# A fifth inner pair in the first down projection, and another order of work around the first norm and in the tail

## The chip, the cores and the metric

One core of a Trainium2 chip runs the whole program once. The metric is the device time of one execution in microseconds (us). The kernel before took 1548.7 us (median of 3 runs, 1547.63 to 1548.96).

## What is computed

One step of a streaming encoder layer over 576 columns (512 frames of a new stream and 64 frames of a running one), model width 1024, hidden width 2816. Cut to what matters here:

```python
h = LN1(alpha*x + 0.5*FFN1(x))                                   # FFN1: (silu(x@Wg) * (x@Wu)) @ Wdown
z = h @ w_in  -> columns split among mLSTM q,k,v,o,i,f | attention q,k,v | branch gates g_m, g_a
h = LN2(alpha*h + w_out(sig(g_m)*P_m(mLSTM(h)) + sig(g_a)*P_a(BandAttn(h))))
y = LN3(alpha*h + 0.5*FFN2(h))
```

All is float32. Each matrix is split into a high part in the format that TensorE multiplies fast (fp32r) and a low part, the rest; a product is three matmuls, high by high, high by low and low by high.

## The kernel before

Everything is kept transposed: a tile is 128 features by 576 tokens. The two halves of the tokens are called A and B (columns 0 to 287 and 288 to 575). TensorE's order is written out by hand (the class `Order` counts the estimated time of the matmuls issued so far, and `later` sets a step due at a time of that count); the orders on ScalarE (ACT), VectorE (DVE), GpSimd (POOL) and SyncE (SP) are made by a scheduler at compile time out of priorities: an instruction counts as issued so many places earlier as its `high_priority` offset says (HOT is 300, the weight pump 30), and `issue_after` puts it behind a named one on the same engine. Every queue is then fixed, and an engine works through its own in order.

**Weights.** `plan` lists the weight chunks in the order of their use. `pump` (L232) loads a chunk into one of two raw buffers (`wr`, an SP transfer), then makes the high part (an ACT copy, `wh`) and the low part (a DVE subtraction, `wl`). There are four pairs of `wh` and `wl` (`NWB`); `done` gives a pair back when the last product with it has been issued. A raw buffer is free for the next load when both parts of its chunk have been made.

**The down projection of an FFN** (`ffn`, from L1290) sums 22 hidden tiles into 8 output tiles j. Hidden tiles 8 to 15, the inner ones, are multiplied for a pair of outputs (j, j+1) with seven block products in place of eight (`seven`, L1154): the blocks are two outputs by two groups of inner tiles (8 to 11 and 12 to 15) by two halves of the tokens. The products are a11, a12, t0, q1, q0, t1 and a22, in the order of the code; their weights stand in four chunks a, t, u and v, the last two made out of sums of the raw chunks. Each product runs over 4 inner tiles with three matmuls each. The other 14 hidden tiles are multiplied one by one (`plain`, L1136) in chunks of 8 and 6 (`DC`). For n = 1 the order is: plain for outputs 1 and 3 together, plain for 5, then for j = 0, 2, 4 `seven` and plain of j, then plain for 6 (half A) and 7, `seven` for 6, and plain for 6 (half B) at the end. `Inner` makes the sums of hidden tiles that the seven products need; `Hidden` makes the high and low parts of the hidden tiles in the order `ORDER`. Both take buffers of the pool `hr` (23 tiles), which holds the raw hidden tiles too.

**The first norm** (`Norm`, L513) collects sums (`take`, `last`), computes mean and variance by small matmuls (`stats`), centres the tiles of one half (`centre`), and finishes tile by tile (`apply`, `finish`). Half A is done while TensorE still works on plain 6; the first products of the next stage follow at once. These are four tiles of w_in taken together (`gemm` with `WAVE_M`, L1777): 48, 40 and 32 (v, k and q of attention's first heads) and "if" (the mLSTM gates, half as much weight, its high and low parts side by side in one `wh` tile). In the first pass the first three are multiplied for half 0 of the tokens, one hidden tile after another, then the fourth, then the same for half 1.

**The tail.** The last norm's last part is `turned` (L703): column sums by small matmuls, rsqrt, then transposes back to token rows, a scaling and the store of `yt`.

Of the kernel before, what the change touches and what calls it, by code (L numbers as in the profile page):

```python
# [11 lines left out]
F32R = mybir.dt.float32r  # L12
# [5 lines left out]
P = 128  # L18
# [70 lines left out]
def tile_layer(ctx: ExitStack, tc: tile.TileContext, ins, outs):  # L89
# [87 lines left out]
    PIECES = {("in", 48), ("in", 40), ("in", 32)}  # L177
# [31 lines left out]
    def split_ds(c):  # L209
# [3 lines left out]
        lo = wpool.tile([P, 1024], F32R, tag="wl", name=nm("wl"), bufs=NWB)  # L213
        a, b = slice(0, 512), slice(512, 1024)
# [17 lines left out]
    def pump(limit=None):  # L232
        limit = limit or wst["ahead"]
        while True:
# [9 lines left out]
            if wst["dma"] < min(len(plan), c + 2):  # L244
                i = wst["dma"]
                if plan[i][1] is None:
                    wst["dma"] += 1
                    continue
# [10 lines left out]
            if c < wst["stop"] and plan[c][0][0][:2] != "ds" and c < wst["taken"] + limit and wst["used"] < NWB:  # L259
# [3 lines left out]
                if plan[c][0] == "if":  # L263
# [4 lines left out]
                    tt(h3[:, :, 64:128], r3, f(h3[:, :, 0:64]), ALU.subtract)  # L268
# [107 lines left out]
    DC = ((0, 8), (8, 8), (16, 6))  # L376
# [5 lines left out]
    def plan_ffn(n):  # L382
# [5 lines left out]
        def chunk(j, c):  # L388
            k0, nk = DC[c]
# [32 lines left out]
    plan_in((48, 40, 32))  # L422
    plan.append(("if", ins["w_if"]))
    plan_in((16, 17))
# [88 lines left out]
    class Norm:  # L513
# [86 lines left out]
        def last(self, j, cc, end=None, behind=None):  # L600
# [6 lines left out]
            tt(s2, s2, sq, ALU.add)  # L607
# [67 lines left out]
        def rsqrt(self, hf, st):  # L675
# [3 lines left out]
            act(m2, st[:, 0:nb], AF.Square)  # L679
# [23 lines left out]
        def turned(self, hf, dh, sq):  # L703
# [11 lines left out]
            for q, s in ((0, s1), (1, self.hs(self.s2, hf)), (0, dh), (1, sq)):  # L715
                for b, a in enumerate(blocks):
                    c = 3 * q + b
                    mm(st[:, c:c + 1], s[:, a:a + P], onec, c == 0 and s is not dh, s is sq and b == nb - 1,
                       skip_group_check=True)
            for s in (s1, dh):  # L720
                mm(mb, ones_d, s, s is s1, s is dh)
# [5 lines left out]
            for q in range(2):  # L727
                for b, a in enumerate(blocks):
# [5 lines left out]
                    n = 256 if q and b == nb - 1 else 512  # L734
# [24 lines left out]
        def apply(self, j, hf, rb):  # L759
# [9 lines left out]
            with tc.high_priority(offset=HOT) if early else nullcontext():  # L769
                with tc.issue_after(self.centred.ins) if early else nullcontext():  # L770
                    stt(dh, dh, g, rb, ALU.mult, ALU.mult)
                self.finish(j, hf, dh, b_)

        def finish(self, j, hf, dh, b_):
            t0, n = self.H[hf]
            if self.final is None:
# [3 lines left out]
                if self.keep:  # L780
                    act(dh, dh, AF.Identity, bias=b_)
                    if self.away is None:
                        SP.dma_start(XD[j][:, t0:t0 + n], dh)
                    act(self.hs(hi, hf), dh)
# [1603 lines left out]
```

## Time and profile before

| | us |
|---|---|
| median of 3 runs | 1548.7 |
| the profiled execution, its own time | 1549.32 |
| its span, first to last instruction | 1547.6 |
| TensorE busy in the span | 1533.9 |
| mean granted TensorE clock, share of 2.4 GHz | 0.998 |

All further numbers are read in the profiled execution; its own time is 0.6 us above the median of the runs. Times of single rows are us from the start of the span, unless "ns" stands there. Engines are PE (TensorE's matmuls), PEld (its weight loads), DVE, ACT, POOL and SP; what stands in square brackets behind a row is the idle time of its engine before it and what ended that.

### The profile page before, as it was taken

The page shows a single profiled execution, that of the slowest core. Times are in us where ns is not written, and L with a number is a line of the kernel's source. Part 1 is how long each engine was busy: PE and PEld are TensorE (multiplying, and loading weights), DVE is VectorE, ACT ScalarE, POOL GpSimd, SP SyncE. Part 2 cuts the span into 40 slices and gives each one's busy share as a digit, 9 for nine tenths or more (in the row PEclk, how much of TensorE's full clock was granted, in tenths as well). Part 3 has the DMA queues.
Part 4 walks back from the last instruction along what each step waited for, and adds up shares of the span by engine and source line. Part 5 has one row for each costly group of instructions (what it writes and reads, how often), then busy time and mean ns, then how long its engine had stood idle before and what let it go on. Part 6 is the DMA issues. An engine that isn't in the chain of part 4 may idle for free.

```text
span 1547.6 us, 29525 instructions
## 1 busy us (share of the span) xinstructions
PE 1533.9 (99%) x11587; PEld 1520.6 (98%) x11587; DVE 1138.0 (74%) x2115; ACT 898.0 (58%) x1714; POOL 227.7 (15%) x430
## 2 busy tenths in 40 slices
PE   9999999999999999999999999999999999999998
PEld 9999999999899999999999999999999999999998
DVE  7877778675869866777586766755776877788765
ACT  7545457433765667777854877753456454457333
POOL 1000000000210015555311223202111000001000
PEclk9999999999999999999999999999999999999999
DMA  8322223533664438687534765642755323226334
GB/s 261 109 104 89 96 96 91 140 102 99 183 172 155 137 137 221 154 208 183 126 130 142 184 146 140 161 144 82 209 145 126 109 82 109 83 71 147 119 113 150
DMA packets 80403, 211.15 MB, mean 136 GB/s; under 512 B 9096, under 2 KB 21256, under 8 KB 80264
## 3 DMA queue, kind: packets, MB, share of 16 engines
q1 hardware_dynamic: 65288, 169.15, 33.3%
q0 software_dynamic: 11808, 34.28, 13.0%
q10 hardware_dynamic: 3168, 5.83, 1.2%
q8 instruction: 91, 1.49, 0.4%
q14 instruction: 48, 0.39, 0.1%
HBM read 172.27 MB, written 21.63 MB: 125 GB/s over the span
## 4 chain that ended last, share of the span: by engine, by line
PE 92%; DVE 3%; ACT 3%; DMA 1%; issue 1%; POOL 0%; SPq 0%; ACTq 0%; DVEq 0%; POOLq 0%
PE mm L135 74%; PE aux L135 16%; PE aux L145 2%; DMA s<-in_xT 1%; ACT sc L149 1%; DVE sc L1645 1%; ACT wh L149 0%; DVE s L152 0%; DMA wr<-in_w_gu 0%; DVE wl L152 0%; ACT s L149 0%; ACT wh L911 0%; DVE s L155 0%; ACT tx L149 0%; DVE tx L152 0%
## 5 line engine op out<-in xcount | busy, mean ns | idle before, releaser
L135 PE MATMUL mm<-s,wh 128*128 128x288 f32 (+2 forms) x3659 | 750.8, 298 | 0.3 <-ACT s L486 0.2
L135 PEld LDWEIGHTS mm<-s,wh 128*128 128x128 f32 x3659 | 588.0, 189 | 3.4 <-ACT s L486 0.5
L135 PE MATMUL mm<-s,wl 128*128 128x288 f32 (+2 forms) x1802 | 532.8, 296 | 3.5 <-DVE wl L152 3.5
L135 PEld LDWEIGHTS mm<-s,wl 128*128 128x128 f32 x1802 | 339.9, 189 | 3.7 <-DVE wl L152 3.7
L149 ACT ACTIVATE wh<-wr 128x1024 fp32r<-128x1024 f32 (+2 forms) x145 | 134.6, 937 | 156.3 <-PE mm L135 82.0
L152 DVE TENSOR_TENSOR wl<-wr,wh 128x1024 fp32r<-128x1024 f32 (+2 forms) x93 | 107.5, 1164 | 50.2 <-ACT wh L149 49.8
L135 PE MATMUL mm<-tx,wh 128*128 128x288 f32 x677 | 140.5, 296 | 0.8 <-DVE tx L152 0.8
L135 PEld LDWEIGHTS mm<-tx,wh 128*128 128x128 f32 x677 | 109.2, 188 | 1.3 <-DVE tx L152 1.0
L135 PE MATMUL mm<-tx,wl 128*128 128x288 f32 x350 | 103.2, 295 | 0.0
L152 DVE TENSOR_TENSOR wl<-wt,wh 128x1024 fp32r<-128x1024 f32 x51 | 63.7, 1250 | 53.4 <-ACT wh L911 53.3
L911 ACT ACTIVATE wh<-wt 128x1024 fp32r<-128x1024 f32 x51 | 54.0, 1059 | 79.4 <-DVE wt L152 79.3
L152 DVE TENSOR_TENSOR wl<-wu,wh 128x1024 fp32r<-128x1024 f32 x63 | 77.0, 1223 | 29.4 <-ACT wh L911 29.4
L911 ACT ACTIVATE wh<-wu 128x1024 fp32r<-128x1024 f32 x63 | 66.7, 1058 | 40.9 <-PE mm L135 35.3
L135 PE MATMUL mm<-tx,ah 128*128 128x288 f32 x416 | 85.1, 296 | 0.0
L197 POOL DMA_DIRECT2D s<-s x16 | 13.7, 856 | 468.8 <-DVE hb L152 426.8
L149 ACT ACTIVATE h<-h 128x288 f32<-128x288 f32 x78 | 34.0, 436 | 60.9 <-DVE h L152 60.9
L152 DVE TENSOR_TENSOR wl<-ws,wh 128x1024 fp32r<-128x1024 f32 x51 | 62.2, 1219 | 8.6 <-ACT wh L911 8.6
L135 PEld LDWEIGHTS mm<-tx,ah 128*128 128x128 f32 x416 | 66.3, 188 | 0.5 <-ACT c L149 0.4
L135 PEld LDWEIGHTS mm<-tx,wl 128*128 128x128 f32 x350 | 65.7, 188 | 0.0
L152 DVE TENSOR_TENSOR ws<-wu 128x1024 f32<-128x1024 f32 (+1 forms) x55 | 64.7, 1176 | 0.0
L135 PE MATMUL mm<-h,wh 128*128 128x288 f32 (+2 forms) x304 | 62.6, 296 | 0.0
L135 PE MATMUL mm<-tx,al 128*128 128x288 f32 x208 | 61.1, 294 | 0.0
(406 smaller groups left out, 3492.3 us busy)
## 6 DMA issues: line engine op xcount, KB each, us to landing
wu<-in_w_gu SPq DMA_DIRECT2D x78, 512.0 KB, 4.3
wr<-in_w_in SPq DMA_DIRECT2D x48, 512.0 KB, 4.2
wr<-in_w_dn SPq DMA_DIRECT2D x37, 512.0 KB, 3.7
wl<-in_w_in POOLq DMA_DIRECT2D x36, 512.0 KB, 6.7
wu<-in_w_in SPq DMA_DIRECT2D x24, 512.0 KB, 4.9
wr<-in_w_dn SPq DMA_DIRECT2D x19, 384.0 KB, 3.6
s<-s POOLq DMA_DIRECT2D x16, 288.0 KB, 4.5
wu<-in_w_ap SPq DMA_DIRECT2D x8, 512.0 KB, 4.7
```

Source lines behind the costliest of these rows:

```text
L135: PE.matmul(out, lhsT, rhs, start=start, stop=stop, **kw)
L145: PE.transpose(out, in_, idn)
L149: return ACT.activation(out, in_, func, **kw)
L152: return (eng or DVE).tensor_tensor(out, a, b, op=op)
L197: return POOL.dma_start(lo, src, accum_op=ALU.add)
L911: self.last = ACT.activation(hi, src, AF.Copy)
L1645: return DVE.tensor_tensor_reduce(out=out, in0=ps, in1=g, op0=ALU.add, op1=ALU.min, scale=1.0, scalar=3e38, accum_out=acc)
```

## The change

1. In the first FFN, hidden tiles 16 and 17 become a fifth inner pair: `seven` runs over 5 tiles per product, plain over 12 tiles (8 and 4). Their weights for a pair of outputs are a fifth chunk "e" (two transfers of 128 KB into a buffer of `hr`, not of `wr`); its seven blocks are made into one `wh` and `wl` pair, which is held until the end of `seven`. `Inner` makes one pair of sums more, in buffers of `hr`. Of the first group of inner tiles, where only half A is used as it is, only that half is split, both parts in one buffer.
2. In the wave behind the first norm "if" is third and 32 fourth, in the plan of the weights too; 32 is converted in one piece, not in two halves.
3. Order on DVE and ACT around the first norm: the whole of `last`, the sum of squares included, stays behind the instruction named; the low parts of the first finished tiles have offset 60, not HOT; the last `take` of tile 6 (half B) comes behind the low part of "if"; the variance of half B comes behind the fourth finished tile's high part.
4. In `turned` the mean's first matmul comes ahead of three of the four column sums, and the last block is scaled and stored in one piece, not in two.

```diff
-    PIECES = {("in", 48), ("in", 40), ("in", 32)}
+    PIECES = {("in", 48), ("in", 40)}
@@ split_ds
+        if what == "e":
+            w = raws.pop(c)
+            r1a, r1b, r2a, r2b = (w[:, i * P:(i + 1) * P] for i in range(4))
+            n = 3 * P
+            act(hi[:, :n], w[:, :n])
+            tt(lo[:, :n], w[:, :n], f(hi[:, :n]), ALU.subtract)
+            tt(r2a, r2a, r2b, ALU.add)
+            tt(r2b, r1b, r2b, ALU.add)
+            tt(r1b, r2a, r1b, ALU.add)
+            tt(r1a, r1b, r1a, ALU.add)
+            act(hi[:, n:7 * P], w[:, :4 * P])
+            tt(lo[:, n:7 * P], w[:, :4 * P], f(hi[:, n:7 * P]), ALU.subtract)
@@ pump
+                if plan[i][0][2:] == ("e",):
+                    if "room" not in ds:
+                        return
+                    raws[i] = ds["room"]()
+                    for e in range(2):
+                        wst["load"] = SP.dma_start(raws[i][:, 2 * P * e:2 * P * (e + 1)], plan[i][1][e])
...
-                    tt(h3[:, :, 64:128], r3, f(h3[:, :, 0:64]), ALU.subtract)
+                    wst["gates"] = tt(h3[:, :, 64:128], r3, f(h3[:, :, 0:64]), ALU.subtract)
@@ the plan
-    DC = ((0, 8), (8, 8), (16, 6))
+    DC = {1: ((0, 8), None, (18, 4)), 2: ((0, 8), (8, 8), (16, 6))}
+    INNER = {1: ((8, 9, 10, 11, 16), (12, 13, 14, 15, 17)), 2: ((8, 9, 10, 11), (12, 13, 14, 15))}
+            if n == 1:
+                plan.append(((f"ds{n}", j, "e"), tuple(ins[f"w_dn{n}"][j + e][:, 16 * P:18 * P] for e in range(2))))
-    plan_in((48, 40, 32))
+    plan_in((48, 40))
     plan.append(("if", ins["w_if"]))
+    plan_in((32,))
@@ Norm
                 tt(s1, s1, d, ALU.add)
-            tt(s2, s2, sq, ALU.add)
+                tt(s2, s2, sq, ALU.add)
...
-            act(m2, st[:, 0:nb], AF.Square)
+            with tc.issue_after(self.fourth.ins) if hf and self.gi == 0 else nullcontext():
+                act(m2, st[:, 0:nb], AF.Square)
@@ Norm.turned
-            for q, s in ((0, s1), (1, self.hs(self.s2, hf)), (0, dh), (1, sq)):
...
+            column(0, s1)
+            mm(mb, ones_d, s1, True, False)
+            column(1, self.hs(self.s2, hf))
+            column(0, dh)
+            column(1, sq)
+            mm(mb, ones_d, dh, False, True)
...
-                    for c in range(0, 512, n):
-                        stt(y[:, c:c + n], pts[b, q][:, c:c + n], rs[:, b:b + 1], self.gb[2 + q][:, c:c + n], ALU.mult, ALU.add)
-                        SP.dma_start(outs["yt"][b, :, q * 512 + c:q * 512 + c + n], y[:, c:c + n])
+                    stt(y, pts[b, q], rs[:, b:b + 1], self.gb[2 + q], ALU.mult, ALU.add)
+                    SP.dma_start(outs["yt"][b, :, q * 512:(q + 1) * 512], y)
@@ Norm.finish
+                    with tc.high_priority(offset=HOT) if early else nullcontext():
+                        act(dh, dh, AF.Identity, bias=b_)
...
+                        x = act(self.hs(hi, hf), dh)
+                    if j == 3 and hf == 0:
+                        self.fourth = x
+                    with tc.high_priority(offset=60) if early else nullcontext():
+                        tt(self.hs(lo, hf), dh, self.hs(f(hi), hf), ALU.subtract)
@@ seven
-            wh, wl = parts[ids[w_]]
-            for i in range(4):
-                ww = slice(c0 + i * P, c0 + (i + 1) * P)
+            for i in range(inner.m):
+                wh, wl = parts[ids[w_ if i < 4 else "e"]]
+                ww = slice(c0 + i * P, c0 + (i + 1) * P) if i < 4 else slice(AT5[what] * P, (AT5[what] + 1) * P)
...
         product(Z, "t1", "b22", False, "t")
+        done(ids["e"])
@@ ffn
-                    ln.take(6, B, Z, ALU.add)
+                    with tc.issue_after(wst["gates"].ins):
+                        ln.take(6, B, Z, ALU.add)
@@ the wave
-    gemm([[(("in", 48), KT)], [(("in", 40), KT)], [(("in", 32), KT)], [("if", KT)]], H,
-         [out_cb(vf0, "v", 0), out_cb(kf0, "k", 0), q0_cb, gate_cb], WAVE_M)
+    gemm([[(("in", 48), KT)], [(("in", 40), KT)], [("if", KT)], [(("in", 32), KT)]], H,
+         [out_cb(vf0, "v", 0), out_cb(kf0, "k", 0), gate_cb, q0_cb], WAVE_M)
```

## Rows read from the trace of the kernel before

**Rows 1.** The page, part 1: busy time, share and instructions of each engine.
```profile
PE 1533.9 (99%) x11587; PEld 1520.6 (98%) x11587; DVE 1138.0 (74%) x2115; ACT 898.0 (58%) x1714; POOL 227.7 (15%) x430
```
**Rows 2.** Windows of 20 us: length, busy (count) per engine, TensorE clock, DMA share, GB/s.
```profile
360.00:380.00 20.00, 20.00 (x154) 20.00 (x153) 11.44 (x17) 5.14 (x6) 0.00 (x0) 1.00 0.27 75
380.00:400.00 20.00, 16.36 (x116) 15.70 (x116) 16.33 (x37) 10.23 (x24) 3.98 (x8) 0.96 0.62 205
400.00:420.00 20.00, 20.00 (x133) 19.61 (x134) 16.62 (x43) 17.98 (x43) 3.02 (x3) 0.87 0.50 141
```
**Rows 3.** PE's longest wait over the span: total us, times, longest.
```profile
PE mm L135 <- DVE wl L152: 3.5, 1, 3.5
```
**Rows 4.** The chain that ended last, a piece of the first down stage.
```profile
278.60 11.11 PE aux L135 x84
```
**Rows 5.** PE in order of time at the first norm: start, us.
```profile
393.53 0.40 PE L135 MATMUL mm<-s,wh 128*128 128x256 f32 x2
397.42 0.39 PE L135 MATMUL mm<-s,wl 128*128 128x256 f32 x1 [3.49 <-DVE wl L152]
...
398.44 2.56 PE L135 MATMUL aux<-onec,s 128*128 128x1 f32 x12
```
**Rows 6.** Windows of 2 us behind that wait, columns as in rows 2.
```profile
398.00:400.00 2.00, 2.00 (x13) 2.00 (x12) 0.81 (x2) 0.39 (x1) 0.00 (x0) 0.56 0.62 201
...
404.00:406.00 2.00, 2.00 (x13) 1.89 (x13) 1.97 (x6) 2.00 (x6) 0.00 (x0) 0.73 0.38 156
```
**Rows 7.** DVE in order of time at the first norm.
```profile
387.34 0.46 DVE L152 TENSOR_TENSOR s<-s,sq 128x288 f32<-128x288 f32 x1 [1.08 <-ACT sq L149]
387.72 1.93 DVE L152 TENSOR_TENSOR s<-s,c 128x288 f32<-128x288 f32 x5
389.56 1.36 DVE L155 SCALAR_TENSOR_TENSOR s<-s,cols,aux 128x288 f32<-128x288 f32 x3
...
394.06 0.45 DVE L152 TENSOR_TENSOR s<-s,mm 128x288 f32<-128x288 f32 x1
...
396.68 1.28 DVE L152 TENSOR_TENSOR wl<-wr,wh 128x512 fp32r<-128x512 f32 x2
```
**Rows 8.** ACT in order of time at the first norm.
```profile
376.62 1.06 ACT L149 ACTIVATE wh<-wr 128x1024 fp32r<-128x1024 f32 x1 [2.52 <-PE aux L135]
...
381.39 0.85 ACT L149 ACTIVATE wh<-wr 128x768 fp32r<-128x768 f32 x1 [3.38 <-issue]
...
382.93 0.63 ACT L149 ACTIVATE wh<-wr 128x512 fp32r<-128x512 f32 x1 [0.36 <-PE mm L135]
...
387.56 1.15 ACT L149 ACTIVATE wh<-wr 128x512 fp32r<-128x512 f32 x2 [0.25 <-DMA wr<-in_w_in]
...
399.61 0.63 ACT L149 ACTIVATE wh<-wr 128x512 fp32r<-128x512 f32 x1 [4.63 <-DMA wr<-in_w_if]
```
**Rows 9.** SP's transfers in order of time at the first norm.
```profile
389.81 2.26 SPq L903 DMA_DIRECT2D wu<-in_w_in  x3
393.84 0.33 SPq L251 DMA_DIRECT2D wr<-in_w_if  x1
```
**Rows 10.** Transfers of pump's line, 374 to 406: issue to landing.
```profile
DMA to landing us min/median/max: 3.5/4.3/5.7
```
**Rows 11.** The same of the next stage's loads (L903), 374 to 406.
```profile
DMA to landing us min/median/max: 4.4/7.2/7.4
```
**Rows 12.** DVE in the first down stage: a wait, and the last hidden low part.
```profile
278.62 0.69 DVE L152 TENSOR_TENSOR h<-wr,wr 128x512 f32<-128x512 f32 x1 [3.76 <-DMA wr<-in_w_dn]
...
291.00 0.76 DVE L152 TENSOR_TENSOR h<-h,h 128x576 fp32r<-128x576 f32 x1
```
**Rows 13.** PE and DVE in order of time in the tail.
```profile
1538.95 1.11 PE L135 MATMUL aux<-s,ones_d 128*128 128x256 f32 x4
...
1541.07 0.47 PE L135 MATMUL aux<-s,s 128*128 128x512 f32 x1 [0.57 <-DVE s L152]
...
1542.96 1.52 DVE L155 SCALAR_TENSOR_TENSOR s<-mm,rs,s 128x512 f32<-128x512 f32 x3
```

More of the change, by code (lines that the diff above doesn't have):

```diff
@@ L713, in turned, with column @@
             s1 = self.hs(self.s1, hf)
-            for q, s in ((0, s1), (1, self.hs(self.s2, hf)), (0, dh), (1, sq)):
+            def column(q, s):
                 for b, a in enumerate(blocks):
                     c = 3 * q + b
[L718 to L721, printed above, removed]
+                    mm(st[:, c:c + 1], s[:, a:a + P], onec, c == 0 and s is s1, s is sq and b == nb - 1, skip_group_check=True)
+            column(0, s1)
[4 more added lines that the diff above has]
+            mm(mb, ones_d, dh, False, True)
             with tc.high_priority(offset=HOT):
@@ L812, in __init__ @@
             self.own = 4
+            self.m = len(raw) // 2
             self.b = {}
@@ L861, in tile_layer, with __init__ @@
     class Inner(Combos):
-        def __init__(self, xs, raw):
+        def __init__(self, xs, raw, inner, more):
             super().__init__(xs, raw, {})
-        def tile(self):
-            return slot(F32R)
+            self.inner, self.more = inner, more
         def part(self, i):
@@ L875, in part @@
             for n, (ka, kb) in ((1, ("t2", "t4")), (0, ("t1", "t3"))):
-                t, hi, lo = self.sums.pop(2 * i + n), self.tile(), self.tile()
+                t = self.sums.pop(2 * i + n)
+                hi, lo = ((slot(F32R) if i < 4 else self.more()) for _ in range(2))
                 act(hi, t)
@@ L1106, in tile_layer, with __init__ @@
     class Hidden(Act):
-        ORDER = (*range(KT), *range(2 * KT, FT), *range(12, 2 * KT), *range(KT, 12))
-        def __init__(self, raw, pools):
+        def __init__(self, raw, pools, inner):
             super().__init__([None] * FT)
             self.raw, self.pools, self.prev, self.n = raw, pools, (None, None), 0
+            second, first = inner
+            self.ORDER = (*(k for k in range(FT) if k not in first + second), *first, *second)
+            self.half = first if len(first) > 4 else ()
         def upto(self, i):
@@ L1118, in upto @@
                 pool, tag, n = self.pools[(i_ >= NH0) + (i_ >= NH1) + (i_ >= FT // 2)]
-                hi, lo = (pool.tile([P, T], F32R, tag=tag, name=nm(tag), bufs=n) for _ in range(2))
+                w = T
+                if j in self.half:
+                    w = HT_
+                    t = pool.tile([P, T], F32R, tag=tag, name=nm(tag), bufs=n)
+                    hi, lo = t[:, :w], t[:, w:]
+                else:
+                    hi, lo = (pool.tile([P, T], F32R, tag=tag, name=nm(tag), bufs=n) for _ in range(2))
                 a, b = self.prev
                 with tc.issue_after(a.ins) if i_ else nullcontext():
-                    a = ACT.activation(hi, self.raw[j], AF.Copy)
+                    a = ACT.activation(hi, self.raw[j][:, :w], AF.Copy)
                 with tc.issue_after(b.ins) if i_ else nullcontext():
-                    b = tt(lo, self.raw[j], f(hi), ALU.subtract)
+                    b = tt(lo, self.raw[j][:, :w], f(hi), ALU.subtract)
                 self.prev = a, b
@@ L1191, in seven @@
             ln.take(j + 1, A, X, ALU.subtract)
+            if "e" in ids:
+                done(ids["e"])
             return Y, Z
@@ L1202, in seven @@
         product(Z, "t1", "b22", False, "t")
+        done(ids["e"])
         return Y, Z
@@ L1300, in ffn @@
                 ds["room"] = lambda: hr.tile([P, T], F32, tag="h", name=nm("h"), bufs=FT + 1)
-                inner = Inner(hp_, [hh[k] for k in range(8, 16)])
-                for i in range(4):
+                inner = Inner(hp_, [hh[k] for ks in INNER[n] for k in ks], INNER[n], lambda: hr.tile([P, T], F32R, tag="h", name=nm("h"), bufs=FT + 1))
+                for i in range(inner.m):
                     later(9000 + 2200 * i, lambda i=i: inner.part(i))
```

39 lines of the change are left out of this document (20 added, 19 removed).

## The prediction

> **What bounds the kernel now.** Three views, in this order. The page's busy line [rows 1] shows TensorE busy for 1533.9 of 1547.6 us, 99%, with DVE at 74% and ACT at 58%: an edit pays only where it takes matmuls away or ends a wait of TensorE. A busy PE is not a PE at its peak, so the second view is the windows: busy share and granted clock together [rows 2]. From 360 to 380 both are full; from 380 to 400 PE is busy for 16.36 us only, and from 400 to 420 it is busy throughout but at 0.87 of its clock. This is the first norm, and the change touches it. The third view, PE's waits, names the cause: its longest by far is one wait of 3.5 us for a weight's low part [rows 3]. In order of time it stands at 393.9: PE has done three matmuls each with tiles 48 and 40 and two with tile 32, and the third, with 32's low part, comes at 397.42 [rows 5]. That low part was made at 396.68, the last of a queue of DVE work [rows 7]. What follows costs as much again: between 398 and about 405 the granted clock is at the lower of its two levels, 1.2 GHz (0.56 of full speed in the first of these windows, 0.73 in the last) [rows 6]. Seven us at half speed are 3.4 us lost. So the place holds 7 us; the rest of the stage has only the matmuls themselves to give.
>
> **Fewer matmuls.** Two hidden tiles by two outputs by two halves by three matmuls are 24 per pair one by one, and 7 products by 3 = 21 in `seven`; four pairs save 12 matmuls. A 128x288 matmul takes 11.11/84 = 132 ns, start to start [rows 4]. Sum: **-1.6 us**, all on the path, since PE has no gap in this stage.
>
> **What the fifth pair costs.** Per pair of outputs DVE and ACT convert 7 small blocks more and 2 by 2 of plain's blocks fewer, with four short adds; `Inner` makes five sums in place of four. DVE, the fuller of the two, is busy for 57% of the 20 us from 360 [rows 2], so the work fits. SP issues two loads more per pair, 0.33 us each [rows 9], into a buffer that no other load waits for, and POOL two accumulating transfers more in all, on an engine busy for 15% [rows 1]. The deadline moves: the first plain part loses 36 matmuls, so `seven` starts 4.8 us sooner. There DVE sat for 3.76 us behind a raw chunk [rows 12], room that the new work can use, and the last hidden low part (291.00 [rows 12]) came so late because its buffer was held by the sums' room; with half tiles for five hidden tiles one buffer more is free. I take 0, with 0 to +1.5 as bounds (one conversion of half a chunk, 0.63 us on ACT [rows 8] and 0.64 on DVE [rows 7], late once).
>
> **The wait at the norm.** I count in the profile's clock with the end of plain 6 (392.8) held fixed. Two resources order the weights: four `wh` pairs and two raw buffers. Before, the pairs of the last `seven` came free one product after another, and ACT took them so: the next plain chunk's 8 tiles at 376.62, its 6 at 381.39, tile 48 at 382.93, tile 40 at 387.56 [rows 8]. Afterwards "e" holds one of the four to the end of `seven`, so each moves one place back: the 8 tiles start at about 381.3, the rest (4 tiles) at 382.9, and 48 and 40 only when t and e come free, at about 387.5. The raw buffers follow: 48's load can be issued when the 8 tiles are converted, about 384.2 (1.06 us on ACT, some 1.3 on DVE, two halves' worth at 0.64 [rows 7], behind two takes), and lands at the shortest 3.5 us later [rows 10], at 387.7. "if" is now third, and its load waits for the buffer that 48 holds until its second low part is made. In the same 5 us DVE has the norm: six centrings of 0.39 us, four tiles finished at 0.45 and two sums (unit prices from [rows 7]), the last two kinds with offset 300 against the pump's 30. From 385.4 this lasts to about 390.4; then come the first low parts and 48's, 0.64 us each half. So 48's raw buffer is free between 391.7 and 393.3, no sooner than the load of "if" left before, 393.84 [rows 9]. That load was converted at 399.61, 5.7 us later [rows 8, 10], behind three 512 KB loads issued from 389.81 on [rows 9], which are still there. With 392.5 + 5.7 + 0.63 (ACT) + 0.7 (DVE) PE goes on at about 399.5. Before, 32 was third and already loaded, and PE went on at 397.42 [rows 5]. Moving "if" forward thus exchanges a wait for DVE for a wait for a load: **+2.1 us**. Bounds: landing in 3.5 us instead [rows 10] gives 397.3, -0.1; with an issue at 393.3 and 5.7 it is 400.3, +2.9.
>
> **The added waits.** The last take of tile 6 stands behind the low part of "if". Behind it in DVE's queue are the sums of half B and all that hangs on them; before it ran at 394.06 [rows 7], now at about 399.6, and the sums end near 401. PE comes to their column sums after one more hidden tile, about 401 too, at half clock later: 0, at most +0.5. The square of half B's mean behind the fourth finished tile costs nothing, as that tile is finished long before. The sum of squares behind the centring frees DVE from its 1.08 us of idling [rows 7]; that hastens the first low parts, which already were in time: 0 here. 32 as fourth and in one piece has 64 matmuls of cover (some 7 us) for a load and 2.3 us of conversion: 0.
>
> The Trainium skill ("DMA: Bandwidth & Descriptors", section "Anatomy of one DMA") puts a transfer at about 2.0 us plus its bytes over 436 GB/s, an estimate of 2.6 us for the gate weights' 256 KB, against 5.7 in this trace. By it PE would go on at about 396.4, and the sum would be 3.1 us lower.
>
> **The clock.** A wait of 3.5 us was followed by the low level [rows 5, 6]; one of 5 to 6 us will be too. I take the same 3.4 us, so 0, with -3.4 (no fall) and +0.5 as bounds.
>
> **The tail.** PE waits for the mean's low part (0.57 us before the product at 1541.07 [rows 13]), and the four ones-matmuls in front of it take 1.11 us; two of them, 0.55 us, move into an earlier wait. Since other steps (the rsqrt, the transposes) follow close, I take half: **-0.3 us** (-0.55 to 0). The last block in one piece saves one start of an instruction, and its store is twice as large: 0.
>
> **The sum**: -1.6 + 2.1 + 0 - 0.3 = +0.2 us on 1549.3, the profiled execution, or 1549.5; that execution stands 0.6 above the median of the runs, so 1548.9 us. The case's own range, with the bounds of the terms, is 1545.5 to 1552.
>
> **Rivals.**
> A: the gate weights come in time. If DVE's queue takes 48's low parts ahead of the finishing tiles (they can be ready near 389, two halves on ACT of 0.58 us after 387.7), "if" is issued at 389.8, lands after 3.5 us at 393.3 [rows 10] and is ready at 394.6: a wait of about 1 us. The clock would stand that: the mean of 0.998 over the span is the one fall above and no other (3.4 of 1547.6 us). The gain is 1.6 + 2.5 + 3.4 + 0.3 = 7.7 us: 1541. For it: nothing but the order stands against it, and less DVE idling shortens the queue. Against it: offset 300 against 30. 0.20.
> A2: the load itself is quick. Issued at 391.7 and landed after the shortest 3.5 us, with 1.3 us of conversion PE goes on at 396.5, 0.9 us sooner than before; with -1.6 and -0.3 that is 1545.9, and 1544.2 if the clock falls for half as long. For it: a quarter of a megabyte is the smallest load here. Against it: the 5.7 us of the same load before [rows 8, 10], and the loads ahead of it are the same. 0.12. (This is the case that the Trainium skill's price of a transfer, above, would make.)
> B, slower: the load of "if" falls behind all four 512 KB loads in SP's queue instead of behind three. These took up to 7.4 us to land [rows 11]; 393.3 + 7.4 + 1.3 is 402, 4.6 us later than before; with -1.6, -0.3 and 0.5 each for the clock and the sums 1552.4. It decides where SP's fixed order has the fourth of them ahead. Against it: before, the fourth left after "if". 0.1.
> C, slower: the held pair delays a chunk in each `seven`. The first plain chunk's conversion can begin only four us before its use, for 2.3 us of work: a margin of 1.7 us; a late raw chunk would cost 1 to 2 us per pair, +4 to +8 with the norm unchanged, 1553 to 1557. Against it: DVE is free there. 0.08.
> D: the change does not do what it says: a conversion late once per pair eats the twelve matmuls and the norm stays as it is: 1548 to 1550, in the same class as the forecast.
>
> **How the numbers follow.** Chances: forecast with D 0.50, A 0.20, A2 0.12, B 0.10, C 0.08. A run of this kernel can tell about 0.2% (3.1 us) from no change. A lies below 1545.6, A2 across it (0.09 of its 0.12 below); B and C lie above 1551.8 for the most part (0.16 of 0.18); of the forecast 0.02 falls on either side. Faster 0.31, same 0.51, slower 0.18. The range takes in A, the forecast and B: 1541 to 1552.5; outside are C and the far half of A.
>
> **What would show it.** Twelve matmuls fewer and full windows from 256 to 390: the first term. In PE's waits the low part of "if" (a DVE subtraction into `wh`) in place of `wl`, with ACT's copy of "if" waiting for its load: the second. If instead 48's low parts stand ahead of the finishing tiles on DVE, it is A. If the granted clock stays at 1.00 through 400, A again. Waits of PE between 280 and 380 mean C. I would be wrong by my own working if the gate weights' load left before 390.

## The result: 6.45 us slower

The changed kernel took 1555.28 us (median of 6 runs, 1553.44 to 1557.61) against 1548.83 for the kernel before (6 runs, 1547.63 to 1550.31) on the same chip: a ratio of 1.004, with a 95% interval of 1.0029 to 1.005. The prediction was 1548.9, with 1541.0 to 1552.5 as its range; the result lies outside it, on the slow side.

The profiled execution of after has a span of 1554.5 us (before 1547.6) and a mean clock of 0.995 (before 0.998). PE executes 11575 matmuls, 12 fewer than in [rows 1], as forecast. The busy line of after's page:

```profile
PE 1536.6 (99%) x11575; PEld 1523.5 (98%) x11575; DVE 1141.8 (73%) x2141; ACT 902.0 (58%) x1725; POOL 227.9 (15%) x432
```

PE's waits over the span of after (total us, times, longest). The first answers to [rows 3]; the other four belong to places where the kernel before does not wait:

```profile
PE mm L135 <- DVE wh L152: 5.4, 1, 5.4
PE mm L135 <- ACT wh L149: 1.2, 1, 1.2
PE aux L135 <- DVE h L152: 1.1, 2, 0.6
...
PE mm L135 <- DVE wl L152: 0.7, 1, 0.7
PE mm L135 <- DVE s L152: 0.5, 1, 0.5
```

**First new place: the first seven products.** PE of after in order of time from 285 on: the row with which the first `seven` starts, the four rows with a wait, and the row with which the second `seven` starts:

```profile
285.27 0.43 PE L135 MATMUL mm<-h,wh 128*128 128x288 f32 x2
...
289.24 0.40 PE L135 MATMUL aux<-h,wh 128*128 128x288 f32 x1 [0.49 <-DVE h L152]
290.52 0.40 PE L135 MATMUL aux<-h,wh 128*128 128x288 f32 x1 [0.61 <-DVE h L152]
292.27 0.53 PE L135 MATMUL mm<-s,wh 128*128 128x288 f32 x2 [1.22 <-ACT wh L149]
293.53 0.40 PE L135 MATMUL mm<-s,wl 128*128 128x288 f32 x1 [0.73 <-DVE wl L152]
...
314.38 0.43 PE L135 MATMUL mm<-h,wh 128*128 128x288 f32 x2
```

Product a12 waits twice for a hidden low part, then t0 for the high and the low part of chunk t: 3.05 us in all. The windows of after behind it (columns as in [rows 2]) show that the clock fell to 1.2 GHz as well:

```profile
292.00:294.00 2.00, 1.00 (x5) 0.77 (x6) 1.75 (x2) 1.68 (x3) 0.00 (x0) 0.99 1.03 261
294.00:296.00 2.00, 2.00 (x10) 2.00 (x9) 1.21 (x2) 0.00 (x0) 0.00 (x0) 0.50 1.00 354
296.00:298.00 2.00, 2.00 (x12) 2.00 (x12) 0.46 (x1) 0.00 (x0) 0.00 (x0) 0.66 1.02 375
```

In the kernel before, the first and the second `seven` start at

```profile
289.54 0.43 PE L135 MATMUL mm<-h,wh 128*128 128x288 f32 x2
...
311.76 0.43 PE L135 MATMUL mm<-h,wh 128*128 128x288 f32 x2
```

so from one start to the next it takes 22.22 us, and after 29.11 (314.38 - 285.27). Nine matmuls more in between (21 in `seven`, 12 fewer in plain 0) are 1.19 us [rows 4]. The place costs 29.11 - 22.22 - 1.19 = **5.7 us**. Of these 3.05 are idle. The three windows hold 3.4 us at 1.2 GHz, which cost about 1.7. The rest, about 0.95, lies around the four waits: the first matmul behind a wait takes about 0.40 us in the rows above, where in the stream one starts 132 ns after the other [rows 4].

**Second place: the norm.** SP, ACT, DVE and PE of after, each in order of time, where the gate weights come in:

```profile
395.63 2.18 SPq L937 DMA_DIRECT2D wu<-in_w_in  x2
397.92 0.37 SPq L273 DMA_DIRECT2D wr<-in_w_if  x1
...
392.42 0.63 ACT L149 ACTIVATE wh<-wr 128x512 fp32r<-128x512 f32 x1 [0.79 <-DMA wr<-in_w_in]
...
403.10 0.63 ACT L149 ACTIVATE wh<-wr 128x512 fp32r<-128x512 f32 x1 [1.76 <-DMA wr<-in_w_if]
...
396.91 0.69 DVE L152 TENSOR_TENSOR wl<-wr,wh 128x512 fp32r<-128x512 f32 x1
...
403.76 0.69 DVE L152 TENSOR_TENSOR wh<-wr,wh 128x512 fp32r<-128x512 f32 x1 [1.66 <-ACT wh L149]
...
404.50 1.22 PE L135 MATMUL mm<-s,wh 128*128 128x256 f32 x4 [5.43 <-DVE wh L152]
...
406.38 0.85 PE L135 MATMUL aux<-onec,s 128*128 128x1 f32 x4
```

48 is converted on ACT from 392.42; its second low part starts on DVE at 396.91; only then is its raw buffer free for "if", whose load leaves at 397.92 and is there at 403. In the kernel before it left at 393.84 [rows 9]. PE waits 5.43 us in place of 3.49 [rows 5]. At the column sums of half B after lies 406.38 - 398.44 [rows 5] = 7.94 us behind before.

| term | us |
|---|---|
| difference up to the start of `seven` (-4.27, where 36 matmuls fewer are -4.75); not traced further | +0.5 |
| twelve matmuls fewer | -1.6 |
| first seven products | +5.7 |
| a wait of 0.55 in plain 6, for a take that frees a PSUM bank | +0.55 |
| wait at the norm, 5.43 - 3.49 | +1.9 |
| longer slow clock behind it (what is left to 7.94) | +0.9 |
| **at the column sums of half B** | **+7.95** |
| from there to the tail | -1.1 |
| in the tail | 0 |

Of the 1.1, 0.8 is a wait of the kernel before in attention that after does not have (for a row maximum, `mx`). The tail is unchanged. PE of before, where the tail starts, and of after:

```profile
1537.24 1.40 PE L135 MATMUL aux<-onec,s 128*128 128x1 f32 x12
```
```profile
1544.06 0.50 PE L135 MATMUL aux<-onec,s 128*128 128x1 f32 x4
...
1547.88 0.47 PE L135 MATMUL aux<-s,s 128*128 128x512 f32 x1 [0.57 <-DVE s L152]
```

From the first column sum to the product behind the mean it takes 3.82 us; before, 3.83 (1537.24 to 1541.07, the latter in [rows 13]), with the same wait of 0.57.

### The profile page after: what moved, and what is told of

Its sections match the earlier page's. It is cut to its first block, busy times and chain, and to the rows that moved or that the text cites. A ratio compares the mean times of both kernels' runs of the same rounds, so it can differ in the third digit from the quotient of the medians.

```text
span 1554.5 us, 29564 instructions
## 1 busy us (share of the span) xinstructions
PE 1536.6 (99%) x11575; PEld 1523.5 (98%) x11575; DVE 1141.8 (73%) x2141; ACT 902.0 (58%) x1725; POOL 227.9 (15%) x432
## 4 chain that ended last, share of the span: by engine, by line
PE 92%; DVE 3%; ACT 3%; issue 1%; DMA 1%; POOL 0%; DVEq 0%; ACTq 0%; POOLq 0%
PE mm L135 75%; PE aux L135 15%; PE aux L145 2%; ACT sc L149 1%; ACT wh L149 1%; DVE sc L1690 1%; DVE wl L152 0%; DVE s L155 0%; ACT s L149 0%; DMA wr<-in_w_if 0%; DVE h L152 0%; DVE s L152 0%; DMA w<-in_w_gu 0%; DVE tx L152 0%; DVE ptl L152 0%
## 5 line engine op out<-in xcount | busy, mean ns | idle before, releaser
L149 ACT ACTIVATE h<-h 128x288 f32<-128x288 f32 (+1 forms) x80 | 35.4, 442 | 61.1 <-DVE h L152 60.9
L135 PE MATMUL mm<-h,wh 128*128 128x288 f32 (+2 forms) x322 | 66.8, 298 | 0.5 <-DVE s L152 0.5
```

Source lines behind the costliest of these rows:

```text
L135: PE.matmul(out, lhsT, rhs, start=start, stop=stop, **kw)
L149: return ACT.activation(out, in_, func, **kw)
```

## Experiments

Two questions: why are the gate weights late at the norm, and why are the operands late at the first `seven`? Ratios are to the kernel before, run on the same chip.

### The norm

**e1: the change without the fifth pair.**

```diff
-    DC = {1: ((0, 8), None, (18, 4)), 2: ...
+    DC = {1: ((0, 8), None, (16, 6)), 2: ...
-    INNER = {1: ((8, 9, 10, 11, 16), (12, 13, 14, 15, 17)), 2: ...
+    INNER = {1: ((8, 9, 10, 11), (12, 13, 14, 15)), 2: ...
...
```

> The changed kernel with the fifth inner pair taken out (22 hidden tiles as before, chunks of 8 and 6, no weight chunk "e"); the order of the norm, the wave and the tail stays as changed. Theory: "e" holds one of four weight pairs, and that alone makes the gate weights' load late. Without it tile 48 is converted some 9 us sooner, the load of "if" leaves by 390 (in the clock of the kernel before), TensorE waits at the norm for under 1.5 us in place of 3.5 and 5.4, the clock stays up, and nothing stalls at the first seven products: 4.5 to 7.5 us faster than before, 1541 to 1544. Rival: the order on VectorE (norm work ahead of 48's low parts) makes the load late by itself: a wait of 3 to 5 us and a time within 2 us of before, 1547 to 1551.

Measured: 1546.75 us, ratio 0.9984 (0.9975 to 0.9993). This is faster than both kernels: 2.5 us under before. The mechanism came as expected: "if" is loaded at 385.71 and PE waits for it for 1.08 us, with no low clock behind it. The gain is below the 4.5 to 7.5 us that were expected. Three waits of 1.9 us together that now show are a part of what is missing. In the profiled execution the clock was low in the tail as well (0.50 from 1540 to 1542, where the kernel before has none). The rest was not traced. PE of e1 at and behind the norm:

```profile
394.56 0.71 PE L135 MATMUL mm<-s,wh 128*128 128x256 f32 x4 [1.08 <-DVE wh L152]
...
402.80 0.38 PE L135 MATMUL mm<-s,wh 128*128 128x256 f32 x1 [1.07 <-DVE s L152]
...
410.68 0.85 PE L135 MATMUL mm<-s,wh 128*128 128x320 f32 x4 [0.69 <-ACT t L149]
```

**e6: e1 with a weight pair held idle in each `seven`.**

```diff
+            act(hi[:, P:P + 2], ident[:, :2])      # the held pair, early
...
+            act(h[:, :P], src[:, 3 * P:4 * P])     # and one block of it late
+                held = n == 1 and i == 3 and what == ("t1" if j == 6 else "a22")
+                wh, wl = parts[ids["e" if held else w_]]
```

> e1_no_fifth (no fifth inner pair, norm and tail as changed), and in each seven products one weight pair is held idle from where "e" would be converted to the end: it gets 2 columns written early, one 128-column block late, and TensorE reads that block in the last product (two small operations of about 0.3 us more per pair of outputs on ScalarE and VectorE each, and no other work of the fifth pair). Theory (the held pair alone makes the gate weights late): tiles 48 and 40 are converted some 5 us later than in e1_no_fifth, the load of "if" leaves 5 us or more later, the wait at the norm grows from 1.1 to 4 to 6 us with low clock behind it: 4 to 7 us slower than e1_no_fifth, 1551 to 1554. At the first seven products, with the old deadline, under 0.5 us. Rival (the fifth pair's conversions on ScalarE and VectorE delay the norm's queue): the wait stays under 2 us, 1546 to 1548.5.

Measured: 1553.14 us, ratio 1.0028 (1.0018 to 1.0038), 6.4 us above e1. The loads of "if" in e1 and in e6, on SP:

```profile
385.71 0.33 SPq L273 DMA_DIRECT2D wr<-in_w_if  x1
```
```profile
395.46 0.33 SPq L268 DMA_DIRECT2D wr<-in_w_if  x1
```

and ACT's conversion of 48 in e1 and in e6:

```profile
382.72 0.63 ACT L149 ACTIVATE wh<-wr 128x512 fp32r<-128x512 f32 x1 [0.36 <-PE mm L135]
```
```profile
389.49 1.13 ACT L149 ACTIVATE wh<-wr 128x512 fp32r<-128x512 f32 x2
```

A pair that does next to nothing moves 48 by 6.8 us and the load by 9.8. A part of this is TensorE's own delay: in e6 the wave starts at 395.93, in e1 3.3 us sooner, at 392.62, and ahead of it e6 has three short waits (0.40, 0.46 and 0.61 us) and low clock behind the last. Counted from the start of the wave, the load leaves 6.9 us ahead of it in e1, 0.5 ahead in e6, and 0.1 behind it in after (397.92 against 397.83). So holding a pair makes up 6.4 of these 7.0 us. PE then waits 3.2 us (4 to 6 was expected) and the clock falls. The held pair, not the fifth pair's work, makes the gate weights late. At the first `seven` PE does not wait at all in e6.

**e3: the change with the raw gate weights in a buffer of `hr`.**

```diff
+                if plan[i][0] == "if":
+                    raws[i] = ds["room"]()
...
```

> The changed kernel with one edit: the raw gate weights ("if") land in a buffer of hr, not in one of the two raw weight buffers, so their load needs not wait until 48 is converted. Theory: the load is what TensorE waits for at the norm; it now leaves with that of 40 and is there by 396; what is left is the conversion behind 40's: wait 1.5 to 2.5 us in place of 5.4, less low clock after it: 3.5 to 6 us faster than the changed kernel, 1549.5 to 1552. Rival: the queue on ScalarE and VectorE is the bound, and the load only happened to end with it: wait over 4 us, 1554 to 1556.

Measured: 1553.68 us, ratio 1.0028 (1.0018 to 1.0038), some 1.9 us better than the change. The load leaves at 370.43, and the wait falls from 5.43 to 1.93 as expected. The time does not reach the expected 1549.5 to 1552. Behind the norm a wait for a finishing tile shows, as in e1, and one of 0.33 us for ACT; a take at the second `seven` adds 0.31. In this execution the clock behind the first `seven` also stayed low for longer than in after (0.50 from 292 to 298). PE of e3:

```profile
413.28 0.38 PE L135 MATMUL mm<-s,wh 128*128 128x256 f32 x1 [0.94 <-DVE s L152]
```

**e10: the order of the wave alone, on the kernel before.**

```diff
-    plan_in((48, 40, 32))
+    plan_in((48, 40))
     plan.append(("if", ins["w_if"]))
+    plan_in((32,))
...
```

> The kernel before with the order of the wave alone (48, 40, if, 32, in the plan of the weights too, 32 in one piece); VectorE's and ScalarE's order at the norm, the tail and the down stage as before. Theory: with four free pairs the load of "if" leaves by 387 as in e1_no_fifth, and its conversion stands behind 40's low parts and the first finished tiles: a wait of 1 to 2.5 us in place of 3.5, the clock mostly up; the gain of e1_no_fifth comes for the most part from here: 1545.5 to 1548. Rival: it comes from the order on VectorE and ScalarE, without which the gate weights' low part is as late as 32's was: 1548 to 1550.

Measured: 1550.3 us, ratio 1.0007 (0.9998 to 1.0016): the rival, by its mechanism and within 0.3 us of its times. The load leaves at 386.22, early enough, but the wait is 3.8 us: DVE makes the low part of "if" at 396.99, behind the last take, the sums and two centrings with offset 300.

**e11: e1 without the added wait.**

```diff
-                    with tc.issue_after(wst["gates"].ins):
-                        ln.take(6, B, Z, ALU.add)
+                    ln.take(6, B, Z, ALU.add)
```

> e1_no_fifth without the added wait: the last take of tile 6, half B, need not stand behind the low part of "if". Theory: the added wait costs about nothing where the gate weights come early: the take runs some 0.5 to 2 us sooner, the low part of "if" 0.45 us later, and the time is within 1 us of e1_no_fifth: 1546 to 1547.5. Rival: the wait delays half B's sums and with them the later finishing tiles (waits of 1.07 and 0.69 us in e1_no_fifth at 402.8 and 410.7): those go, 1 to 2 us faster, 1544.5 to 1546.

Measured: 1549.48 us, ratio 1.0002 (0.9994 to 1.0011), 2.7 us slower than e1; neither theory allowed for that. DVE of e1, then of e11:

```profile
393.73 0.68 DVE L152 TENSOR_TENSOR wh<-wr,wh 128x512 fp32r<-128x512 f32 x1
394.33 0.45 DVE L152 TENSOR_TENSOR s<-s,mm 128x288 f32<-128x288 f32 x1
```
```profile
393.02 0.45 DVE L152 TENSOR_TENSOR s<-s,mm 128x288 f32<-128x288 f32 x1 [0.47 <-PE mm L135]
393.39 1.19 DVE L152 TENSOR_TENSOR s<-s,s 128x288 fp32r<-128x288 f32 x3
...
396.12 0.68 DVE L152 TENSOR_TENSOR wh<-wr,wh 128x512 fp32r<-128x512 f32 x1
```

Without the wait, the take (offset 300) pulls all that hangs on it ahead of the gate weights (offset 30): their low part comes 2.4 us later, and PE waits 3.26 us in place of 1.08. The added wait is what makes the new wave order pay; e10 lacks it too.

### The first seven products

**e2: the fifth pair alone, on the kernel before.** All other edits are undone (the wave, the norm's order, the tail).

```diff
-    plan_in((48, 40))
-    plan.append(("if", ins["w_if"]))
-    plan_in((32,))
+    plan_in((48, 40, 32))
+    plan.append(("if", ins["w_if"]))
...
```

> The kernel before with the fifth inner pair alone; wave, norm and tail ordered as before. Theory: the stall at the first seven products (3.05 us idle and some 2.65 us of low clock in the changed kernel) comes from the fifth pair: 5.7 - 1.6 for the matmuls = +4.1, and the held weight pair delays 48, 40 and 32 at the norm by 0 to 2 us more: 1553 to 1555. Rival: the stall is a product of the other edits or of chance in the order: no wait over 0.5 us between 280 and 300, 1546.5 to 1548.5.

Measured: 1557.86 us, ratio 1.0055 (1.0043 to 1.0068). The same four waits stand at 288 to 294 (0.60, 0.61, 1.22, 0.41), so they belong to the fifth pair. The norm was worse than expected, and with it the time: 1.67 us for 40's low part and 3.44 for 32's high part.

**e4: sums and hidden splits due sooner.**

```diff
-                    later(9000 + 2200 * i, lambda i=i: inner.part(i))
+                    later(9000 + (1500 if n == 1 else 2200) * i, lambda i=i: inner.part(i))
-                    later(15000 + 1500 * i, lambda i=i: hp_.upto(14 + i))
+                    later((10500 if n == 1 else 15000) + (1000 if n == 1 else 1500) * i, ...
```

> The changed kernel with one edit: in the first down stage the sums of the inner tiles and the splits of the last hidden tiles are due sooner (9000 + 1500 i in place of 9000 + 2200 i, and 10500 + 1000 i in place of 15000 + 1500 i, in estimated ns of TensorE), so they stand earlier in the fixed queues. No work is added or taken away. Theory: the stall at the first seven products is one of order, a deadline moved by 4.3 us under queues that were laid out for the old one; the idle time there falls from 3.05 us to under 1, the clock stays up: 4 to 5.7 us faster than the changed kernel, 1549.5 to 1551.5. Rival: the added work itself (conversion of "e", a fifth pair of sums) fills VectorE and ScalarE: the stall stays over 2 us, 1554 to 1556.

Measured: 1555.45 us, ratio 1.0037 (1.0023 to 1.0051), the time of the change. The hidden parts were in time, but the wait went to the next operand: 2.75 us for t's high part and 0.41 for its low part. This seemed to speak for the rival, but DVE showed another reason: t's four sums stood behind the last hidden splits, since the first needs a buffer of `hr`, and one comes free only with such a split.

**e8 and e5: t's first sum in the raw buffer of "e"** (in e8 alone, in e5 with e4's due times).

```diff
+            ds["ew"] = w
...
-            q = ds["q"] = ds["room"]()[:, :512]
+            q = ds["q"] = (ds.pop("ew") if "ew" in ds else ds["room"]())[:, :512]
```

> The changed kernel with one half of e5_sums_sooner: the first sum for chunk "t" goes into the raw buffer of "e"; the due times stay. Theory: t's weights come in time but the last hidden low parts stay where they were or later: of the idle time at 284 to 294 some 2 us stay (waits for a hidden tile's low part), with low clock behind them: 0 to 3 us faster than the changed kernel, 1552.5 to 1555.5. Rival (t's weights alone were the bound): under 0.8 us idle, 1549.5 to 1551.5.

Measured: 1557.72 us, ratio 1.0053 (1.0041 to 1.0066). At the first products it is as expected: three waits for hidden low parts, 1.95 us, and none for t. But the second `seven` gained a wait of 1.45 us for a take, because its sums must now wait for the conversion of "e"; the time did not get better, and lies above both expected ranges.

> The changed kernel with two edits in the first down stage: the due times of e4_sooner, and the first sum for chunk "t" is written into the raw buffer of "e" (dead by then) instead of a fresh buffer of hr. In e4_sooner the last hidden parts came in time, but chunk t's sums stood behind them on VectorE, since their fresh buffer of hr comes free only with a hidden tile's split; now they need no buffer. No work is added. Theory (a deadline 4.3 us sooner against queues tied by order and by the full hr): both late things, the hidden low parts and t's weights, are early enough; the idle time between 284 and 294 falls from 3.05 to under 0.8 us and the clock stays up: 4 to 5.5 us faster than the changed kernel, 1549.5 to 1551.5. Rival (the work of the fifth pair fills VectorE): another operand is late in their place, over 2 us idle, 1554 to 1556.

Measured: 1553.24 us, ratio 1.003 (1.002 to 1.0039). The first products are mended: one wait of 0.77 us is left and the clock stays up. PE of e5:

```profile
289.06 0.50 PE L135 MATMUL mm<-s,wh 128*128 128x288 f32 x2 [0.77 <-DVE s L155]
```

The median gains only 2 us of the 4 to 5.5 and lies between the two expected ranges; the profiled execution, 1551.54, gains more. A wait of 0.84 us for a take shows at the second `seven`. What the other executions lose was not seen. Each half by itself leaves the stall (3.16 us of waits in e4, 1.95 in e8); both together end it but for the 0.77, with all work of the fifth pair kept.

**e14 and e13: the deadline without the work, and the deadline with less of it.**

```diff
-    DC = {1: ((0, 8), None, (16, 6)), 2: ...      (e14, on e1)
+    DC = {1: ((0, 8), None, (18, 4)), 2: ...
...
-            n = 3 * P                              (e13, on the change)
+            n = 4 * P
-            tt(r2a, r2a, r2b, ALU.add)
-            tt(r2b, r1b, r2b, ALU.add)
-            tt(r1b, r2a, r1b, ALU.add)
-            tt(r1a, r1b, r1a, ALU.add)
```

> e1_no_fifth with hidden tiles 16 and 17 left out of the first down projection altogether (their share of the outputs is left out of what is computed; 96 matmuls fewer): the first seven products start 36 matmuls, 4.75 us, sooner, as in the changed kernel, but nothing of the fifth pair is there, no "e", no fifth sums, no held pair. Theory (the deadline alone): a wait for a hidden low part or for t's weights of 2 us or more stands at the first seven products, since in the kernel before the last hidden low part was made only 0.5 us before its use; 12.7 us less for the matmuls and some 3 to 5 lost there: 1537 to 1539. Rival (it takes the fifth pair's work or its buffers): under 0.8 us idle there, 1533 to 1535.

Measured: 1540.35 us (3 runs). `seven` starts at 284.46, and all that waits is

```profile
287.86 0.40 PE L135 MATMUL aux<-h,wh 128*128 128x288 f32 x1 [0.35 <-DVE h L152]
```

My theory of the deadline falls: 4.75 us less cost 0.35 us here. t's sums start on DVE at 277.48, right behind the low part of the chunk before; nothing of the fifth pair stands ahead of them. (The time lies above both expected ranges; at the norm stand a wait of 2.4 us and low clock.)

> The changed kernel with less work for "e": its four sums and its second conversion are left out (the products t0, q1 and q0 take the blocks of a12, a11 and a22 instead, so the fifth pair's share of them is left out of what is computed); the deadline, the held pair and all buffers stay. Theory (deadline and order): the hidden low parts and t's weights stand where they stood or some 1 to 2 us earlier, and over 1.5 us of the 3.05 idle at 284 to 294 stays, with low clock behind it: 0 to 3 us faster than the changed kernel, 1552.5 to 1555.5. Rival (the added conversions fill ScalarE and VectorE): under 0.8 us idle, full clock, 1549.5 to 1551.5.

Measured: 1556.39 us, ratio 1.0045 (1.0026 to 1.0065). Three waits, 3.03 us, stay at 289 to 293, and the time is even above the expected range: the sums of "e" and its second conversion are not it either. What is left of the fifth pair is its hidden sums with their splits, the first conversion, the buffers of `hr` and the steps that are queued for them. No run takes these apart; but e5 keeps all that work, changes due times and one buffer, and the stall goes. So it is order and buffers that decide.

**e12: e5 with the fifth pair in the first three `seven` only.** Tile 17 must then be split whole, in two buffers of `hr`, not one.

```diff
+    def dc(n, c, j):
+        return (16, 6) if n == 1 and c == 2 and j >= 6 else DC[n][c]
-            for i in range(inner.m):
+            for i in range(4 if j == 6 else inner.m):
...
-            self.half = first if len(first) > 4 else ()
+            self.half = first[:4] if len(first) > 4 else ()
...
```

> e5_sums_sooner with the fifth inner pair in the first three seven products only; outputs 6 and 7 multiply tiles 16 and 17 one by one, so no "e" holds a weight pair when the norm's weights are converted (nine matmuls fewer than before, not twelve; tile 17 is split whole). Theory (the last "e" alone makes the gate weights late): the norm looks as in e1_no_fifth, a wait of about 1.1 us and no low clock behind it: e1_no_fifth's time less 1.2 for the matmuls plus 0.8 to 2 for the waits left at the first and second seven products: 1546 to 1548. Rival (the sooner due times or the late first seven products shift the norm's queue as well): a wait over 3 us there, 1551 to 1554.

Measured: 1551.48 us, ratio 1.0018 (1.0009 to 1.0026). The wait at the norm is as expected: 1.08 us, as in e1. But the clock did not stay up behind it:

```profile
402.00:404.00 2.00, 2.00 (x8) 1.71 (x8) 1.44 (x5) 1.01 (x4) 1.00 (x1) 0.50 1.00 410
```

The time is far above the expected 1546 to 1548, for the first products, which e5 had mended, stall again, and the second `seven` waits 1.26 us for a take. PE of e12:

```profile
291.33 0.40 PE L135 MATMUL aux<-h,wh 128*128 128x288 f32 x1 [2.82 <-DVE h L152]
```

One buffer of `hr` less (and half a split more, 0.3 us) brings back 2.8 us of wait. What the trace shows is order. The last hidden low part on DVE, in e5 and in e12:

```profile
286.67 0.75 DVE L152 TENSOR_TENSOR h<-h,h 128x576 fp32r<-128x576 f32 x1
```
```profile
290.52 0.76 DVE L152 TENSOR_TENSOR h<-h,h 128x576 fp32r<-128x576 f32 x1
```

In e5 it stands ahead of the conversions of the weights, in e12 behind three of them (286.90 to 290.5). That the missing buffer is what put it there is likely, but not shown by itself.

### Both places mended

**e7: e5 with e3's edit. e9: the same, but only the first `seven` takes the buffer of "e".**

```diff
-            ds["ew"] = w
+            if plan[c][0][1] == 0:
+                ds["ew"] = w
```

> e5_sums_sooner with the edit of e3_gates_room as well (raw gate weights in a buffer of hr): both places of loss mended, the fifth pair and its twelve matmuls fewer kept. Theory: the two gains add, 4 to 5.5 and 1.6 to 2: 1547.5 to 1549.5, the time of the kernel before. Rival: mending one lets the next wait show (a later operand of the first products, the finishing tiles at the norm): 1551 to 1554.

Measured: 1550.45 us, ratio 1.0008 (0.9999 to 1.0017), between the two expected ranges. Waits for takes are left at the first `seven` (1.06 us) and at the second (1.53 us), and 1.93 us at the norm.

> e7_sums_gates with one difference: only the first seven products take the raw buffer of "e" for chunk t's first sum, the later ones a fresh buffer of hr as in the changed kernel. In e5, e7 and e8 the second seven products gained a wait of 0.8 to 1.5 us for a take on VectorE at 337 to 342, since there the sums for t could start only when "e" had been converted. Theory: that wait goes, the rest stays as in e7: 1 to 1.5 us faster than e7, 1548.5 to 1549.5. Rival: the wait comes from the sooner due times: e7's time, 1550 to 1551.

Measured: 1548.01 us, ratio 0.9995 (0.9987 to 1.0004). Between 284 and 384 PE has no wait at all. Against the kernel before, run on the same chip, the change stood 6.45 us above and e9 stands 0.7 us below: two buffers and the due times take back the whole loss, so the two places were the loss. A clear gain over before it is not (the interval takes in 1). PE of e9 at the norm, where "e" still holds its pair:

```profile
395.22 0.73 PE L135 MATMUL mm<-s,wh 128*128 128x256 f32 x4 [1.93 <-DVE wh L152]
```

Low clock follows, and three smaller waits (0.55 in plain 6; 0.74 and 0.33 behind the norm) that the kernel before does not have. A pair of its own for "e" was not tried.

## Why the prediction was wrong

**Right.** The twelve matmuls: twelve fewer are counted, and -1.6 is their number times their price; no run measures them alone. The norm: +1.9 us of wait where +2.1 was forecast, by the mechanism of the text, which e6 shows alone: held pair, 48 later, its raw buffer later, the load of "if" later (issue 5.1 us before it was there; 5.7 was taken). The signs named for it, a subtraction into `wh` and ACT waiting for the load, stand in the rows of after above. The load of "if" left behind two of the four 512 KB loads, so B did not come, and it took 5.1 us to land, so A2 did not either. The Trainium skill's price of a transfer ("DMA: Bandwidth & Descriptors", section "Anatomy of one DMA", which gives it for transfers that GpSimd issues, where this load leaves from SP), an estimate of 2.6 us, is near e6's 2.9 us and not near after's 5.1 us. In both runs the load left behind two 512 KB loads of SP issued within 2.6 us ahead, so what makes the difference is not shown.

**The step that failed** stands under "What the fifth pair costs": "I take 0, with 0 to +1.5 as bounds". It measured 5.7. Two sentences carried it, and both fell. "With half tiles for five hidden tiles one buffer more is free": the five half tiles save five buffers of `hr`, but "e" takes one and the fifth pair's sums four, so by this count none is left over; e12, with one more in use, stalls again. "There DVE sat for 3.76 us behind a raw chunk, room that the new work can use" [rows 12]: idle time of an engine that goes through its queue in order is room only for what may stand there. ACT of after, then DVE of after on the way to t's low part:

```profile
279.96 0.63 ACT L149 ACTIVATE wh<-h 128x512 fp32r<-128x512 f32 x1 [2.81 <-DVE h L152]
...
283.08 2.73 ACT L1164 ACTIVATE h<-h 128x288 fp32r<-128x288 f32 x5
```
```profile
280.62 0.69 DVE L152 TENSOR_TENSOR wl<-h,wh 128x512 fp32r<-128x512 f32 x1 [0.33 <-ACT wh L149]
283.54 2.00 DVE L152 TENSOR_TENSOR h<-h,h 128x288 fp32r<-128x288 f32 x3 [2.22 <-ACT h L1164]
...
286.85 0.69 DVE L152 TENSOR_TENSOR h<-wr,wr 128x512 f32<-128x512 f32 x1
...
290.38 0.69 DVE L152 TENSOR_TENSOR wr<-wr 128x512 f32<-128x512 f32 x1
292.25 1.23 DVE L152 TENSOR_TENSOR wl<-wr,wh 128x1024 fp32r<-128x1024 f32 x1 [1.18 <-ACT wh L149]
```

DVE idles 2.22 us for the hidden copies, which stand on ACT behind the second conversion of "e" and the fifth sums' splits (279.96 to 283.1); t's first sum comes at 286.85, once a buffer is free, where it ran at 278.62 before [rows 12]. The price of the bound was also wrong in kind: one late conversion, but no clock. Behind 3.05 us of idle time came 3.4 us at 1.2 GHz, which cost 1.7 more (the 2.65 us named in the expectation of e2 take in the 0.95 around the waits).

**Mis-sized.** The clock at the norm: 0 taken, +0.5 as upper bound, about +0.9 measured. The tail: -0.3 taken, 0 measured; PE runs through from the first column sum to the mean's last matmul, so there was no earlier wait into which matmuls could move. The added wait of the last take: 0 in the change, as forecast, but worth 2.7 us where the weights are early (e11). The bank wait of 0.55 us in plain 6 was not seen; it stands in each kernel here with the fifth pair in the last `seven`, and in none without. Two sums were off as well, by little: the bounds of the terms add up to about 1543 to 1552.5, not to the 1545.5 to 1552 that were given, and A's gain is 7.8 us, not 7.7.

**Rivals.** C's time (1553 to 1557) came true, and its sign, waits between 280 and 380, but by luck: the waits stood in the first `seven` only, where the held pair was not the cause. e6 holds a pair and does not wait there, and e9 mends the place with the pair still held. A's condition, gate weights in time, holds in e1; its gain without the matmuls was put at 6.1 us and measured 2.5, in part since DVE's finishing tiles are the next bound. D, a conversion late once per pair with the norm as it was, did not come. With a chance of 0.08 for C, the range ended 2.8 us too low.

## What to carry over

Before idle time of an engine is counted as room for new work, look at what the work must stand behind in that engine's queue, and which buffer it needs: count the tiles of the pool at its fullest point, not on the average. A tile that is held longer from a small rotating set moves every later load that waits for a place in it; here one pair of four moved a load by 9.8 us, or by 6.4 against the products that wait for it (e6). And an order by priorities must be followed to the end: a moved chunk gains only if what overtakes it is tied down as well (e10, e11).

## What was not expected of the hardware

The granted clock does not follow the length of one wait alone. Behind a wait of 1.93 us at 395 in e9, of 1.53 us at 339 in e7 and of 0.55 us at 390 in e8, in this order, the windows were

```profile
396.00:398.00 2.00, 2.00 (x12) 2.00 (x10) 1.11 (x3) 0.01 (x1) 0.00 (x0) 0.50 0.93 326
```
```profile
340.00:342.00 2.00, 2.00 (x17) 2.00 (x17) 1.00 (x2) 0.00 (x0) 0.00 (x0) 1.00 0.78 243
```
```profile
390.00:392.00 2.00, 2.00 (x9) 2.00 (x10) 2.00 (x6) 1.09 (x4) 0.00 (x0) 0.50 0.91 266
```

that is 1.2, 2.4 and 1.2 GHz. The same wait of 0.55 us at 390 in after left the clock up:

```profile
390.00:392.00 2.00, 1.54 (x11) 1.54 (x12) 2.00 (x5) 1.24 (x4) 0.36 (x1) 1.00 0.64 242
```

In both kernels the same work stands ahead of it, the twelve small column sums of the norm and a few matmuls, so this does not tell them apart. In the same way a wait of 1.08 us at the norm left the clock up in e1, and in e12 it was low some 2.4 us behind it. What tells these cases apart was not tried.
